# Scale and offset of X behind chosen loads, roped queries turned behind the keys, silu ahead of additions, first token tile finished first

## The chip, the cores and the metric

One Trainium2 chip, one core of it. The metric is the time of one execution on the device, in microseconds (us), as the median of several runs. The engines are TensorE (PE; its weight loads, PEld, overlap the matmuls), VectorE (DVE), ScalarE (ACT), GpSimd (POOL) and SyncE (SP), which only issues transfers.

## The reference

Two layers over 256 tokens of width 2048. Each mixes tokens with eight heads of latent attention and 1024 channels of causal convolution side by side, projects both with one matrix, and then applies a squared-ReLU MLP of width 8192. A layer norm stands before the layers and after each half of a layer.

```python
def hybrid_layer(x, cos, sin, ...):
    z = x @ w_in
    c_q, c_kv, k_rope, u = z[..., :o1], z[..., o1:o2], z[..., o2:o3], z[..., o3:]
    q = (rms_norm(c_q, g_q) @ w_uq).reshape(B, S, MLA_HEADS, QK_NOPE + QK_ROPE)
    q_nope = q[..., :QK_NOPE]
    q_rope = apply_rope(q[..., QK_NOPE:], cos[:, :, None, :], sin[:, :, None, :])
    kv = (rms_norm(c_kv, g_kv) @ w_ukv).reshape(B, S, MLA_HEADS, QK_NOPE + V_HEAD)
    k_nope, v = kv[..., :QK_NOPE], kv[..., QK_NOPE:]
    k_rope = apply_rope(k_rope, cos, sin)
    attn = chunk_causal_mla(q_nope, q_rope, k_nope, k_rope, v).reshape(B, S, MLA_WIDTH)
    u = u + b_glu
    h = u[..., :CONV_WIDTH] * jax.nn.sigmoid(u[..., CONV_WIDTH:])
    h = causal_depthwise_conv(h, w_dw, b_dw)                 # 31 taps
    h = jax.nn.silu(layer_norm(h, g_cln, b_cln))
    mix = jnp.concatenate([attn, h], axis=-1) @ w_out
    x = layer_norm(ALPHA * x + mix, ln1_g, ln1_b)
    f = jnp.square(jax.nn.relu(x @ w1)) @ w2
    return layer_norm(ALPHA * x + f, ln2_g, ln2_b)

def reference(x, ...):
    h = layer_norm(x, ln_in_g, ln_in_b)
    for l in range(DEPTH):
        h = hybrid_layer(h, ...)
    return h
```

## The kernel before

X, the activations, stays in SBUF as two token tiles (t = 0, 1) of 128 tokens by 2048; a block n of it is 512 columns. All weights come from HBM once, in chunks of up to 1 MB, in the order of `chunk_order` (line 193): per layer the convolution inputs u(0) to u(3), between them the query and key/value latents (zq, zk), the roped and plain query parts (qr, qn), keys (kn), values (v), then the projection wo in two halves (k0 = 0 takes the attention result mx, k0 = 8 the convolution result mc), then w1 and w2.

Each matmul in fp32 is made of three with operands cut into a high and a low part. So a chunk is loaded into `wr` (`load_next`, line 234, SP's queue), ACT rounds it to `wh` (line 264) and VectorE or GpSimd subtracts to get the low half `wl` (line 265, which is line 93 where VectorE does it). `gpsimd_low` (line 42) says whose work it is: GpSimd's for most of what lies before the MLP. A chunk is 24 matmuls of 512 columns for `wo` (12 a token tile) and 48 of 256 columns for u. `get` and `retire` pace loads and cuts by what TensorE has used up: a few chunks ahead (`ahead`), at most `cap` loaded and not given back.

The program text isn't the order of the queues. The compiler of this language simulates all engines and puts each instruction into its engine's queue when it would be ready there; after that each queue runs in order, and an instruction that waits holds what stands behind it. `tc.issue_after(ins)` puts the instructions of its block behind `ins` where they are on the same engine. It does nothing else.

The places that matter here:

- **The input norm** (`class First`, line 470). Its scale and offset are first applied to the transposed copy only (`gain`). `rest(n)` (line 491) applies them to X itself later, for the sum after the projection: for scale and then offset it issues a broadcast of 512 numbers to all partitions on SP and two GpSimd operations on X. It is called for n = 0 to 3 after the key rope, within the keys, after the values and after the attention of layer 0 (lines 853, 923, 928, 999).
- **rstd_of** (line 354) makes each norm's reciprocal root: a VectorE step (vi, vq, vk, vc, va, vb), then a power on GpSimd (ri, rq, rk, rc, ra, rb).
- **Latents** (`rms_T`, line 778): squares on ACT, `rstd_of`, the normalised latents `cnq` on VectorE, turned by TensorE (cTq).
- **query_rope** (line 870): VectorE ropes the queries of each token tile into `rt`, TensorE turns them (qrT). It stands before the plain queries and the keys (`keys`, line 882).
- **conv_norm** (line 1013): the convolution output is turned, normalised (`yt`, after rc), turned back in four groups (`cp`, yT), and ACT and VectorE make the silu and cut it into mc. It is written before blocks 2 and 3 of the projection's first half.
- **close** (line 701): the last part of a sum, with the statistics of the following norm. In its last block token tile 0 is done first, `between` starts tile 0's norm, then tile 1 runs; the norm of tile 1 follows. Block 2 of tile 0, and blocks 1 to 3 of tile 1 (in the very last norm block 3 alone), are scaled on ACT and GpSimd (`nrm`, line 393); the rest is two VectorE operations on X.
- **PSUM banks** (lines 122 to 150): ring `mm` for sums, `ax` for turnings, two for the convolution. In the MLP `mm` has six.

## Time and profile before

| | |
|---|---|
| median of 3 runs | 2053.14 us (2051.37 to 2055.04) |
| profiled execution, on the device | 2048.13 us |
| its span, first to last instruction | 2046.3 us |
| TensorE busy | 1995.7 us (98%) |
| VectorE, ACT, GpSimd busy | 1235.9, 949.2, 361.6 us |
| moved by DMA | 377.67 MB, 185 GB/s in the mean |

Times in the rows below are from the span's start. Layer 0 runs from about 48 to 1035 us; the MLPs of both layers fill most of the span. A matmul's row shows its modelled length; matmuls overlap, so the rate is read from a stretch with their count.

### The profile page before, as it was taken

What the parts mean: (1) busy time and instruction counts of PE and PEld (TensorE: products, weight loads), DVE (VectorE), ACT (ScalarE), POOL (GpSimd) and SP (SyncE); (2) the same over time, 40 slices, a digit from 0 to 9 for tenths busy, and PEclk for the clock granted to TensorE, in tenths of its full rate; (3) what the DMA queues carried; (4) which work ended last, traced back from release to release, by engine and by line L of the source; (5) the groups of instructions that cost most, each with busy time, mean ns of one, the idle gap of its engine ahead of it and who ended that gap; (6) DMA issues with size and microseconds to landing.
All of it is one profiled execution on the core that took longest, in us unless ns stands there. A gap on an engine that the chain in (4) does not pass through costs nothing. (4 is left out here: it accounts for less than half of the span.)

```text
span 2046.3 us, 26177 instructions
## 1 busy us (share of the span) xinstructions
PE 1995.7 (98%) x10542; PEld 1706.2 (83%) x10542; DVE 1235.9 (60%) x1709; ACT 949.2 (46%) x1343; POOL 361.6 (18%) x224
## 2 busy tenths in 40 slices
PE   8899999999999999999999999999999999999997
PEld 5799877888888888888879997788888888888886
DVE  6776677554555555456567746875555545555564
ACT  5446555543453354345345564554444434543441
POOL 6496602000000000000038763200000000000001
PEclk8899999999999999999999999999999999999999
DMA  8565645566556645656556455455664565556561
GB/s 249 154 177 163 206 167 180 169 196 202 177 185 197 220 159 185 215 170 246 170 165 176 125 183 206 165 185 168 202 220 151 188 202 186 186 187 225 197 213 62
DMA packets 226170, 377.67 MB, mean 185 GB/s; under 512 B 15955, under 2 KB 70083, under 8 KB 225025
## 3 DMA queue, kind: packets, MB, share of 16 engines
q1 hardware_dynamic: 225696, 375.47, 56.3%
q8 instruction: 82, 1.34, 0.3%
q10 hardware_dynamic: 352, 0.54, 0.1%
q14 instruction: 40, 0.32, 0.1%
HBM read 373.88 MB, written 2.10 MB: 184 GB/s over the span
## 5 line engine op out<-in xcount | busy, mean ns | idle before, releaser
L264 ACT CAST wh<-wr 128x1024 fp32r<-128x1024 f32 (+2 forms) x700 | 684.8, 1031 | 727.9 <-DVE wl L93 323.3
L93 DVE TENSOR_TENSOR wl<-wr,wh 128x1024 fp32r<-128x1024 f32 x576 | 686.4, 1235 | 432.7 <-ACT wh L264 299.1
L93 PE MATMUL f<-xTa,wh 128*128 128x512 f32 x1920 | 676.8, 397 | 0.0
L93 PE MATMUL w<-wh,h 128*128 128x512 f32 x2048 | 632.2, 389 | 2.5 <-DVE f115s L93 1.4
L93 PE MATMUL f<-xTa,wl 128*128 128x256 f32 x1920 | 538.0, 281 | 0.0
L93 PEld LDWEIGHTS w<-wh,h 128*128 128x128 f32 x2048 | 384.4, 188 | 83.1 <-DVE f115s L93 1.7
L93 PEld LDWEIGHTS f<-xTa,wh 128*128 128x128 f32 x1920 | 360.4, 188 | 87.6
L93 PE MATMUL w<-wl,h 128*128 128x512 f32 x1024 | 398.4, 389 | 0.0
L93 PEld LDWEIGHTS f<-xTa,wl 128*128 128x128 f32 x1920 | 362.7, 189 | 0.9
L265 POOL TENSOR_TENSOR wl<-wr,wh 128x1024 fp32r<-128x1024 f32 (+2 forms) x124 | 268.2, 2187 | 92.8 <-ACT wh L264 44.4
L358 POOL TENSOR_TENSOR rb<-vb,mhalf 128x1 f32<-128x1 f32 x4 | 4.2, 1049 | 1396.8 <-DVE nmub L93 1396.8
L93 PEld LDWEIGHTS w<-wl,h 128*128 128x128 f32 x1024 | 192.2, 188 | 39.6
L93 DVE SCALAR_TENSOR_TENSOR cv<-hg,wdT,cv 128x255 f32<-128x255 f32 (+14 forms) x480 | 187.1, 466 | 9.3 <-ACT cv L639 9.3
L93 PE MATMUL wo<-wh,mc 128*128 128x512 f32 x256 | 82.6, 402 | 3.5 <-ACT mc L171 3.5
L93 PE MATMUL wo<-wh,mx 128*128 128x512 f32 x256 | 82.0, 396 | 1.1 <-ACT mx L171 1.1
L93 DVE TENSOR_TENSOR X<-X,w 128x512 f32<-128x512 f32 x48 | 33.0, 688 | 68.0 <-PE w L93 67.9
L93 PE MATMUL u<-xTi,wh 128*128 128x256 f32 x384 | 72.5, 289 | 0.3 <-DVE rbk L93 0.3
L93 PE MATMUL u<-xTb,wh 128*128 128x256 f32 x384 | 71.1, 286 | 0.0
L93 PEld LDWEIGHTS wo<-wh,mc 128*128 128x128 f32 x256 | 49.6, 194 | 15.0 <-ACT mc L171 4.5
L93 PEld LDWEIGHTS u<-xTi,wh 128*128 128x128 f32 x384 | 61.3, 195 | 0.7 <-DVE rbk L93 0.6
L93 PEld LDWEIGHTS u<-xTb,wh 128*128 128x128 f32 x384 | 60.2, 191 | 0.2
L93 PEld LDWEIGHTS wo<-wh,mx 128*128 128x128 f32 x256 | 47.8, 188 | 11.5 <-ACT mx L171 1.5
(400 smaller groups left out, 1837.0 us busy)
## 6 DMA issues: line engine op xcount, KB each, us to landing
wr<-in_w_dram SPq DMA_DIRECT2D x256, 1024.0 KB, 5.2
wr<-in_w_out_dram SPq DMA_DIRECT2D x32, 1024.0 KB, 5.4
wr<-in_w_in_dram SPq DMA_DIRECT2D x60, 512.0 KB, 6.1
wr<-in_w_in_dram SPq DMA_DIRECT2D x8, 1024.0 KB, 10.4
wr<-in_w_uq_dram SPq DMA_DIRECT2D x24, 256.0 KB, 4.3
wr<-in_w_in_dram SPq DMA_DIRECT2D x8, 640.0 KB, 4.4
wr<-in_w_ukv_dram SPq DMA_DIRECT2D x8, 512.0 KB, 5.1
wr<-in_w_in_dram SPq DMA_DIRECT2D x16, 128.0 KB, 5.1
```

The source lines that it names most:

```text
L93: return f(*args, **kw)
L264: nc.scalar.copy(hi[:, c], raw[:, c])
L265: eng.tensor_sub(lo[:, c], raw[:, c], hi[:, c].bitcast(F32))
L358: nc.gpsimd.tensor_tensor(out=r, in0=v, in1=mhalf, op=ALU.pow)
```

## The change

- `gpsimd_low`: the low halves of layer 0's first u group are VectorE's, no longer GpSimd's.
- `rest`: called later (after the values, after u(3), and twice within the projection's first half); its broadcasts issue behind the latest weight load, its GpSimd operations behind GpSimd's latest low half at that place of the program.
- The roped queries of token tile 0 are turned behind the last matmul of the keys' first half, those of tile 1 behind the second.
- Projection, first half, block 3: the second chunk's matmuls for token tile 0 issue behind the turning of silu group 1, those for tile 1 behind that of group 2; the block's additions issue behind the cut of group 1 on VectorE.
- Projection, second half: blocks 2 and 3 are interleaved so that token tile 0 is finished first. Token tile 0 of block 3 ends 36 matmuls before the end; it was 24.
- The very last sum: token tile 1 is added up in PSUM (four banks, `end`) and normalised from there; of its blocks GpSimd takes block 2 and not block 3.

```diff
     if tag == "u":
-        return key[2] >= 2 - l or (l, key[2]) == (0, 0)
+        return key[2] >= 2 - l
...
-                nc.sync.dma_start(sl(rv), ap)
+                last["load"] = nc.sync.dma_start(sl(rv), ap)
...
-                eng.tensor_sub(lo[:, c], raw[:, c], hi[:, c].bitcast(F32))
+                low = eng.tensor_sub(lo[:, c], raw[:, c], hi[:, c].bitcast(F32))
+                if eng is nc.gpsimd:
+                    last["low"] = low
...
+        def source(self, t, n):
+
+            return self.inp.get((t, n), X[:, t, n * 512:(n + 1) * 512])
...
-                eng.scalar_tensor_tensor(out=X[:, t, c], in0=X[:, t, c], scalar=m[:, 0:1], in1=self.g[:, c],
+                eng.scalar_tensor_tensor(out=a, in0=a, scalar=m[:, 0:1], in1=self.g[:, c],
                                          op0=ALU.subtract, op1=ALU.mult)
-                eng.scalar_tensor_tensor(out=X[:, t, c], in0=X[:, t, c], scalar=r, in1=self.b[:, c],
+                eng.scalar_tensor_tensor(out=X[:, t, c], in0=a, scalar=r, in1=self.b[:, c],
                                          op0=ALU.mult, op1=ALU.add)
...
-                nc.sync.dma_start(w, ap[c].partition_broadcast(P))
-                for t in range(2):
-                    nc.gpsimd.tensor_tensor(out=X[:, t, c], in0=X[:, t, c], in1=w, op=op)
+                with tc.issue_after(last["load"].ins):
+                    nc.sync.dma_start(w, ap[c].partition_broadcast(P))
+                with tc.issue_after(last["low"].ins):
+                    for t in range(2):
+                        nc.gpsimd.tensor_tensor(out=X[:, t, c], in0=X[:, t, c], in1=w, op=op)
...
+        elif t and N is not None and N.last:
+            vector.tensor_add(ps[t], X[:, t, c], ps[t])
+            N.inp[t, n] = ps[t]
         else:
             vector.tensor_add(X[:, t, c], X[:, t, c], ps[t])
...
+            pc, pd = out_banks(tag, l, k0, 2), [psum(f"{tag}{l}_{k0}_3_0")]
+            out_part(pc, tag, l, k0, 2, 0, act, False)
+            out_part(pc, tag, l, k0, 2, 1, act, True, (0,))
+            accumulate(0, pc, 2, first, N)
+            for kc in range(2):
+                out_part(pd, tag, l, k0, 3, kc, act, kc == 1, (0,))
+            between(0, pd)
+            pd.append(psum(f"{tag}{l}_{k0}_3_1"))
+            out_part(pc, tag, l, k0, 2, 1, act, True, (1,))
+            accumulate(1, pc, 2, first, N)
+            out_part(pd, tag, l, k0, 3, 0, act, False, (1,))
+            out_part(pd, tag, l, k0, 3, 1, act, True, (1,), lambda: between(1, pd))
+            accumulate(1, pd, 3, first, N)
         N.head(1)
-        for n in range(3 if N.last else 1, NC4):
-            N.nrm(1, n, nc.gpsimd)
+        for n in range(1, NC4):
+            if not N.last or n == 2:
+                N.nrm(1, n, nc.gpsimd)
...
-        beside(query_rope())
+        def query_turn(t, after):
+            ps = psumx(f"qrT{l}{t}")
+            with tc.issue_after(after.ins):
                 for k in range(4):
-                    tensor.transpose(ps[:, k * P:(k + 1) * P], rt[:, k * P:(k + 1) * P], ident)
-                nc.scalar.copy(qr[:, :, t * P:(t + 1) * P], v3(ps, 4))
+                    tensor.transpose(ps[:, k * P:(k + 1) * P], rt[t][:, k * P:(k + 1) * P], ident)
+            nc.scalar.copy(qr[:, :, t * P:(t + 1) * P], v3(ps, 4))
+        query_rope()
...
         queries(0)
-        keys(0)
-        if l == 0:
-            N.rest(1)
-        keys(4)
+        query_turn(0, keys(0))
+        query_turn(1, keys(4))
         values(0)
         values(1)
         if l == 0:
-            N.rest(2)
+            N.rest(0)
         queries(4)
...
         beside(attention((0, 1, 2, 3)))
+        u_group(3)
         if l == 0:
-            N.rest(3)
-        u_group(3)
+            N.rest(1)
...
         out_part(pa, "wo", l, 0, 0, 1, mixT, True)
+        if l == 0:
+            N.rest(2)
...
+        if l == 0:
+            N.rest(3)
+        flush()
+        beside(conv_norm())
+        ps = out_rows("wo", l, 0, 2, mixT)
+        for t in range(2):
+            accumulate(t, ps, 2, True)
+        ps = out_banks("wo", l, 0, 3)
+        out_part(ps, "wo", l, 0, 3, 0, mixT, False)
+        with tc.issue_after(turned[1].ins):
+            out_part(ps, "wo", l, 0, 3, 1, mixT, True, (0,))
+        with tc.issue_after(turned[2].ins):
+            out_part(ps, "wo", l, 0, 3, 1, mixT, True, (1,))
+        with tc.issue_after(silus[1].ins):
             for t in range(2):
-                accumulate(t, ps, n, True)
+                accumulate(t, ps, 3, True)
...
-                give_back()
+                if N.last:
+                    banks["end"] = banks["mm"][2:]
+                    del banks["mm"][2:]
+                else:
+                    give_back()
                 close("w2", l, q * 16, act, N)
```

## Rows read from the trace of the kernel before

**Rows 1.** The page: busy us, share of the span, instructions, by engine.

```profile
PE 1995.7 (98%) x10542; PEld 1706.2 (83%) x10542; DVE 1235.9 (60%) x1709; ACT 949.2 (46%) x1343; POOL 361.6 (18%) x224
```

**Rows 2.** Waits of TensorE: waiter <- releaser: us in total, times, longest.

```profile
PE cTq L93 <- DVE cnq L93: 9.4, 1, 9.4
PE tri L93 <- DVE xv L93: 5.7, 3, 3.4
PE qrT L93 <- DVE rt L93: 4.8, 2, 2.4
PE wo L93 <- ACT mc L171: 3.5, 4, 1.2
PE f L93 <- DVE xTa L93: 2.2, 2, 1.1
PE yT L93 <- ACT zz L1041: 1.8, 2, 0.9
PE u L93 <- POOL wl L265: 1.6, 2, 0.9
...
PE tra L93 <- DVE X L93: 1.2, 2, 0.6
```

**Rows 3.** VectorE's timeline: start, us, line, operation, count, idle before.

```profile
74.38 0.14 DVE L93 TENSOR_SCALAR vq<-ssq 128x1 f32<-128x1 f32 x1
...
85.72 0.75 DVE L93 SCALAR_TENSOR_TENSOR cnq<-zq,rq,gq 128x512 f32<-128x512 f32 x1 [7.47 <-POOL rq L358]
```

**Rows 4.** GpSimd's timeline, same columns, 58 to 96 us.

```profile
58.66 3.66 POOL L497 TENSOR_TENSOR X<-X,gi 128x512 f32<-128x512 f32 x2 [9.55 <-DMA gi<-in_ln_in_g_dram]
...
82.67 2.48 POOL L497 TENSOR_TENSOR X<-X,bi 128x512 f32<-128x512 f32 x2 [4.07 <-DMA bi<-in_ln_in_b_dram]
85.11 0.57 POOL L358 TENSOR_TENSOR rq<-vq,mhalf 128x1 f32<-128x1 f32 x1
```

**Rows 5.** Stretches: engines' busy us (instructions), granted clock, DMA share, GB/s.

```profile
86.62:90.10 3.48, 3.48 (x17) 3.48 (x18) 2.95 (x7) 0.59 (x1) 1.79 (x2) 0.50 0.18 58
...
271.00:274.40 3.40, 3.40 (x9) 2.61 (x8) 2.54 (x3) 3.39 (x6) 0.00 (x0) 0.50 0.09 33
```

**Rows 6.** GpSimd's timeline, first half of layer 0's projection.

```profile
232.53 19.03 POOL L265 TENSOR_TENSOR wl<-wr,wh 128x1024 fp32r<-128x1024 f32 x8 [3.82 <-ACT wh L264]
254.81 1.07 POOL L358 TENSOR_TENSOR rc<-vc,mhalf 128x1 f32<-128x1 f32 x2 [3.25 <-DVE vc L93]
```

**Rows 7.** Stretch of the first half of the projection, wo alone.

```profile
233.94:251.10 17.16, 17.16 (x75) 14.00 (x75) 2.73 (x4) 1.00 0.92 311
```

**Rows 8.** TensorE's timeline at the roped queries and at the silu.

```profile
160.13 0.66 PE L93 MATMUL qrT<-ident,rt 128*128 128x128 f32 x4 [2.38 <-DVE rt L93]
...
267.29 0.60 PE L93 MATMUL yT<-ident,yt 128*128 128x128 f32 x4
```

**Rows 9.** Stretch of one half of the keys, instructions on kn alone.

```profile
160.98:163.90 2.92, 2.92 (x24) 2.87 (x25) 0.21 (x1) 1.00 0.51 123
```

**Rows 10.** VectorE's timeline, the convolution norm's last output.

```profile
257.44 1.52 DVE L93 TENSOR_SCALAR yt<-cT,cmv,rc 128x512 f32<-128x512 f32 x2
```

**Rows 11.** VectorE's timeline at the end.

```profile
2036.39 2.07 DVE L93 SCALAR_TENSOR_TENSOR X<-X,mvb,gb 128x512 f32<-128x512 f32 x3
2038.38 4.08 DVE L93 SCALAR_TENSOR_TENSOR X<-X,rb,bb 128x512 f32<-128x512 f32 x3
```

**Rows 12.** GpSimd's timeline at the end.

```profile
2038.37 1.87 POOL L403 TENSOR_TENSOR X<-X,gb 128x512 f32<-128x512 f32 x1 [0.83 <-ACT X L402]
2040.32 1.59 POOL L404 TENSOR_TENSOR X<-X,bb 128x512 f32<-128x512 f32 x1
```

**Rows 13.** VectorE's timeline in the head.

```profile
19.12 5.91 DVE L93 TENSOR_SCALAR X<-X,mvi,ri 128x512 f32<-128x512 f32 x4 [0.68 <-POOL ri L358]
...
44.31 2.36 DVE L93 TENSOR_TENSOR wl<-wr,wh 128x1024 fp32r<-128x1024 f32 x2 [5.71 <-ACT wh L264]
```

**Rows 14.** ACT's timeline at the end of the head.

```profile
43.23 2.00 ACT L264 CAST wh<-wr 128x1024 fp32r<-128x1024 f32 x2 [6.89 <-DMA wr<-in_w_in_dram]
```

More of the change, by code (lines that the diff above doesn't have):

```diff
@@ L230, in hybrid_trunk @@
     index = {k: i for i, (k, _) in enumerate(plan)}
-    raws, ready, cut_after = {}, {}, {}
+    raws, ready, cut_after, last = {}, {}, {}, {}
     state = dict(loaded=0, cut=0, retired=0, ahead=1, cap=5, hold=False, gate=None, pieces=2)
@@ L330, in stat_w @@
                              skip_group_check=True)
-            tensor.matmul(o, lhsT=lo[:, ki, c], rhs=act[:, 0:S], start=False, stop=last,
-                             skip_group_check=True)
+            done = tensor.matmul(o, lhsT=lo[:, ki, c], rhs=act[:, 0:S], start=False, stop=last,
+                                 skip_group_check=True)
+        return done
     def stat_w2(o, hi, lo, ki, m, act, first, last):
@@ L365, in __init__ @@
             self.mv = {}
+            self.inp = {}
             self.done = set()
@@ L652, in out_banks, with out_part @@
     def out_banks(tag, l, k0, n):
-        return [psum(f"{tag}{l}_{k0}_{n}_{t}") for t in range(2)]
-    def out_part(ps, tag, l, k0, n, kc, act, last, tokens=(0, 1)):
+        return [turns(f"{tag}{l}_{k0}_{n}_{t}", "end" if t and "end" in banks else "mm") for t in range(2)]
+    def out_part(ps, tag, l, k0, n, kc, act, last, tokens=(0, 1), amid=None):
         hi, lo = get(tag, l, k0, n, kc)
@@ L663, in out_part @@
                         retire(tag, l, k0, n, kc)
+                    if amid is not None and ki == 1:
+                        amid()
                     tick()
@@ L711, in between @@
                 N.turn(0, 0)
-        for n in range(NC4):
-            end = n == NC4 - 1
-            ps = out_rows(tag, l, k0, n, act, (3 if N.last else 2) if end else 0, between)
-            for t in range(2):
-                if t or not end:
-                    accumulate(t, ps, n, first, N)
+        if len(act) > 2:
+            for n in range(NC4):
+                end = n == NC4 - 1
+                ps = out_rows(tag, l, k0, n, act, (3 if N.last else 2) if end else 0, between)
+                for t in range(2):
+                    if t or not end:
+                        accumulate(t, ps, n, first, N)
+        else:
+            for n in range(NC4 - 2):
+                ps = out_rows(tag, l, k0, n, act)
+                for t in range(2):
+                    accumulate(t, ps, n, first, N)
+            pc, pd = out_banks(tag, l, k0, 2), [psum(f"{tag}{l}_{k0}_3_0")]
[11 more added lines that the diff above has]
+            accumulate(1, pd, 3, first, N)
         N.head(1)
-        for n in range(3 if N.last else 1, NC4):
-            N.nrm(1, n, nc.gpsimd)
+        for n in range(1, NC4):
+            if not N.last or n == 2:
+                N.nrm(1, n, nc.gpsimd)
     for l in range(L):
@@ L851, in hybrid_trunk @@
         beside(key_rope())
-        if l == 0:
-            N.rest(0)
         u_group(2)
@@ L868, in hybrid_trunk @@
         retire("qr", l)
+        rt = []
         def query_rope():
             for t in range(2):
[L872 to L875 removed]
+                rt.append(work(f"rt{l}{t}", "ev", 4))
+                rope(v3(rt[t], H), v3(pq[t], H), t, H, f"q{l}{t}")
+        def query_turn(t, after):
+            ps = psumx(f"qrT{l}{t}")
+            with tc.issue_after(after.ins):
                 for k in range(4):
[L877 to L880 removed]
+                    tensor.transpose(ps[:, k * P:(k + 1) * P], rt[t][:, k * P:(k + 1) * P], ident)
+            nc.scalar.copy(qr[:, :, t * P:(t + 1) * P], v3(ps, 4))
+        query_rope()
         def keys(h0):
@@ L1011, in cuts_after @@
                 cut_after[i] = ins
+        turned, silus = [], []
         def conv_norm():
@@ L1042, in conv_norm @@
                                          scale=pH[:, l, 16 + c:17 + c])
+                turned.append(tr)
                 yield 1
@@ L1064, in hybrid_trunk @@
             accumulate(t, pb, 1, True)
-        for n in range(2, NC4):
-            if n == 2:
-                flush()
-                beside(conv_norm())
-            ps = out_rows("wo", l, 0, n, mixT)
+        if l == 0:
[3 more added lines that the diff above has]
+        ps = out_rows("wo", l, 0, 2, mixT)
+        for t in range(2):
+            accumulate(t, ps, 2, True)
[6 more added lines that the diff above has]
+        with tc.issue_after(silus[1].ins):
             for t in range(2):
-                accumulate(t, ps, n, True)
+                accumulate(t, ps, 3, True)
         flush()
```

27 lines of the change are left out of this document (13 added, 14 removed).

## The prediction

> **What bounds the kernel now.** The first view is the page: TensorE is busy 1995.7 us, 98% of the span of 2046.3 us [rows 1]. No other engine comes near, and the matrix work itself is not touched by the change, so all there is to win is time in which TensorE waits, stretches in which it works at its lower clock, and the ends. The second view is the list of TensorE's waits [rows 2]. One is long, 9.4 us in a single piece before the turned query latents (cTq). Behind it come three waits for xv at the start (5.7 us), two of 2.4 us for the roped queries (4.8 us), 3.5 + 1.8 us where the silu of the convolution half feeds the projection, 2.2 + 1.2 us between projection and MLP, and 1.6 us for low halves made by GpSimd. The third views are the timelines around each, to see who was late and why. The last is the end, where TensorE has nothing left and the rest is VectorE, GpSimd and the output [rows 11, 12].
>
> The profiled execution took 2048.13 us, 1.8 us more than its span and 5.0 us less than the median of the runs, 2053.14 us. The sum below is made against the profiled execution; the same difference is then taken off the median.
>
> **Scale and offset of X (the rest calls).** The cause of the 9.4 us is on GpSimd. VectorE has the variance sum (vq) ready at 74.38 us [rows 3], but the tiny power (rq, 0.57 us) runs at 85.11 us, because the multiply and add of X by scale and offset stand before it in GpSimd's queue and wait there for their broadcasts, up to 9.55 us for one [rows 4]. Afterwards TensorE works at half clock: granted 0.50, the 1.2 GHz level, from 86.62 to 90.10 us [rows 5]. Work that takes 3.48 us there takes 1.74 at the other level. The change puts each of the eight broadcasts behind a given weight load and the sixteen GpSimd operations behind a given low half, far later. rq can then start at 74.5 and end near 75.1, the normalised latents (cnq, 0.75 us [rows 3]) near 75.9 plus what VectorE is in the middle of, which is before TensorE asks at 77.2 (86.62 less 9.41). Gain: 9.4 + 1.7 = 11.1 us. With GpSimd rid of this work, its low halves for the u group behind the key/value latents no longer run late, and the 1.6 us [rows 2] go too.
>
> What was moved must now be paid somewhere: sixteen operations at 1.24 us (2.48 for two, [rows 4]), 19.8 us of GpSimd, half before the projection, where nothing close by waits for it, half within the first half of layer 0's projection. There GpSimd makes eight low-half operations back to back, 19.03 us from 232.53 [rows 6], so it ends at 251.56. Projection matmuls go at 17.16 / 75 = 0.229 us [rows 7], so the last of the eight weight chunks, 24 matmuls, is begun at 267.29 - 5.5 = 261.8 [rows 8]. The lead is 10.2 us, the added work there 8 x 1.24 = 9.9. It fits, barely, if no broadcast is late. Behind it in the queue is the power of the convolution's norm (rc, now at 254.81 [rows 6]) and behind that the transposes. I price this at 2 us, between 0 and the 9.9 of the rival below, nearer to 0 because rc can be queued between two low halves.
>
> **Roped queries.** TensorE stands 2.38 us before the second turning in each layer [rows 8], waiting for VectorE's rope. Now the turnings come after the first and second half of the keys. One half is 24 matmuls, 2.92 us [rows 9], more than the wait. The keys' low half and latents are older than the rope. Gain 4.8 us in all; if the keys were late, 0. The scores use the turned queries only after the values; that slack I read from the order of the code.
>
> **Silu.** After the last projection matmul of the attention half TensorE turns the convolution output at 267.29 us [rows 8], then waits for ACT, 1.8 us in all before transposes and 3.5 us before the matmuls on the silu's result, over both layers [rows 2]; and from 271.0 the clock granted is 0.50 for 3.40 us [rows 5], 1.7 us lost; there are two such stretches, one a layer. The convolution norm's output is there at 258.96 (257.44 + 1.52 [rows 10]), but part of the transposes sit behind all of the matmuls. Now the second pair is turned before the last quarter-block of 12 matmuls of token tile 0 and the third before those of tile 1, so ACT has two times 12 x 0.229 = 2.7 us of cover more; and VectorE must do the silu before it adds the last projection block. The bank that this addition frees is next written 12 matmuls into the new half, so the wait is covered. Full gain 5.3 + 3.4 = 8.7; less the 2 us above, 6.7. Bounds: 8.7, and below nothing, as the rivals tell, because TensorE can now be held by a transpose whose input is late.
>
> **Projection, token tile first.** The two blocks of the second half are reordered so that all of token tile 0 ends 36 matmuls before the end and not 24: 2.7 us more for its addition, statistics and scaling. The waits for it are 1.2 us (X) and 2.2 us (xTa) [rows 2]. I take 2.4 of the 3.4, since VectorE must still turn to token tile 1 in the same stretch; bounds 0 and 3.4. One weight chunk is given back 24 matmuls later, 5.5 us; the loads that this holds up on SP are those of the MLP's third chunk, used over 5 us after the end.
>
> **The tail.** Three additions of the offset take 4.08 us where three multiplications took 2.07 [rows 11], while GpSimd works on X beside them (1.87 and 1.59 us [rows 12], against 1.24 undisturbed). With tile 1's sum kept in PSUM, VectorE reads one operand there. By [rows 11] six operations of 0.69 from 2036.39 end at 2040.5, not 2042.5; GpSimd at its undisturbed speed ends at 2038.37 + 2.48 = 2040.9, not 2041.9. The later of the two is 2040.9, gain 1.5 us; bounds 0.5 (only the GpSimd end left) and 2.0. The third block goes to GpSimd in place of the fourth, with no effect on the sum. The Trainium skill (SBUF — State Buffer, Who interferes with whom) says that a VectorE instruction with two SBUF inputs and a GpSimd instruction that reads SBUF exclude each other, and one with a single SBUF input does not. By that rule the whole 1.5 us come; the 4.08 against 2.07 agrees.
>
> **The head.** The sixteen low halves of the first u group go from GpSimd to VectorE. At 2.36 us for two of twice the size [rows 13] they cost 0.59 each, 9.4 us on an engine that is nearly full there. Against it, VectorE's own operations slow beside GpSimd: four scalings of X took 5.91 us, 1.48 each [rows 13], where 0.59 is the price of a clean operation of that size with one input more. That gives back 3.6 us on these four, and as much is likely on the other four and on the eight splits. So the two nearly cancel. Bounds: gain of the 5.7 us of waits for xv [rows 2], or a loss of 9.4. I take a gain of 1, near the middle, because ACT has to wait for the next weights until 43.23 us anyway [rows 14]. The Trainium skill (VectorE: DVE Perf Modes, Mode 2×_2P) gives such a scaling two results a cycle, an estimate of 0.27 us each; by it the relief would be 4.8 us on the same four and the sum 1 or 2 us lower. No row shows one without GpSimd beside it.
>
> **Sum.** 11.1 + 1.6 + 4.8 + 6.7 + 2.4 + 1.5 + 1.0 = 29.1 us. Profiled execution 2048.1 - 29.1 = 2019.0; median 2053.1 - 29.1 = **2024.0 us**.
>
> **The rivals.**
> - *GpSimd's moved work holds the projection.* All eight of its operations stand before rc: rc comes at 254.81 + 9.9 = 264.7, the norm's output at 268.9, and TensorE, now bound to those transposes at 261.8, waits 7.1 us; layer 0's silu gain (2.7 after the price) is gone as well. 2024 + 9.8 = 2034. For it: the lead of 10.2 against 9.9. Against: layer 1 has no such work, and rc can slip in earlier. Chance 0.17.
> - *The head pays.* VectorE gets no relief and TensorE waits for the low halves, 9.4 lost and not 1 won: 2034. For it: VectorE has hardly an idle moment there. Chance 0.11.
> - *The long stall only moves.* With cTq in time the next limit is the supply of weights: a second half-load of that stretch was issued late as well, behind the same broadcasts. If half of the 11.1 stays, 2030. Chance 0.08; it lies inside the range.
> - *Slower than before.* The broadcasts are issued from SP, behind weight loads that wait for buffers; GpSimd would stand before low halves as it stood before rq. Four broadcasts in layer 0's projection at 9.55 each and 9.9 of work are 48.1 us, less the lead of 10.2: 37.9 us lost, 2062. It decides against the change from 7.4 us a broadcast on (29.1 + 10.2 - 9.9 over four). Chance 0.05: the loads there run well ahead.
>
> **How the numbers follow.** Forecast 0.57, rivals 0.17, 0.11, 0.08, 0.05, something not seen 0.02. Low end: all waits named go, 11.1 + 1.6 + 4.8 + 8.7 + 3.4 + 2.0 + 5.7 = 37.3, so 2016, and 2 us less for the spread of the runs: 2014. High end: the first two rivals together, 2024 + 9.8 + 10.4 = 2044. About 0.2% (4 us) is what a measurement of this kernel can tell from no change. Faster: 0.92; same 0.02; slower 0.06.
>
> **What would show it.** Right: no idle time before cTq, rq within 2 us of vq; no clock of 0.50 near 87 and 271 us; no wait of qrT on rt; the offset additions at the end at 0.7 us. Wrong: TensorE waiting for wl from GpSimd or for yt near 260 us; xv or wl waits before 45 us longer than now; rest operations waiting for broadcasts with low halves behind them.

## The result and the profile after

The changed kernel takes **2028.7 us** (median of 4 runs, 2028.1 to 2029.9) beside 2052.3 us for the kernel before on the same chip (4 runs, 2050.8 to 2055.0). The ratio is 0.9884, with a 95% interval from 0.9867 to 0.9901: 23.6 us gained, where 29.1 were forecast. The time lies 4.7 us above the forecast of 2024.0.

The profiled executions stand closer together: span 2046.3 us before, 2027.7 us after, 18.7 us less. The profiled execution of before was 4 us faster than its median, that of after 1.2 us slower. So the sizes below, which come from the two traces, add up to 18.7; the other 4.9 us lie between these two executions and the medians.

TensorE is busy 1993.4 us and has the same work as before. The first six rows of the list of its waits (waiter <- releaser: us in total, times, longest):

```profile
engine line waited for: us in total, times, longest us
PE tri L93 <- DVE xv L93: 7.5, 2, 4.3
PE yT L93 <- ACT zz L1080: 2.2, 4, 0.9
PE prmT L93 <- ACT xv L497: 2.0, 1, 2.0
PE pv L93 <- ACT pts L1019: 1.9, 1, 1.9
PE f L93 <- DVE xTa L93: 1.6, 2, 1.0
PE w L93 <- DVE f015s L93: 1.5, 1, 1.5
```

Beside [rows 2], the long wait before cTq, the waits for the roped queries, for mc and for GpSimd's low halves are gone. The waits for xv have grown from 5.7 to 7.5 us, and two have come: prmT on ACT (2.0) and pv on ACT (1.9, before 0.2). The wait of yT on ACT has grown from 1.8 to 2.2.

The granted clock, in three stretches (busy us with instructions of each engine, then clock, DMA share, GB/s):

```profile
core 0: us, PE busy (x) PEld busy (x) DVE busy (x) ACT busy (x) POOL busy (x), PEclk, DMA share, GB/s
27.48:37.72 10.24, 6.25 (x21) 5.08 (x22) 9.37 (x21) 7.74 (x20) 2.90 (x8) 0.50 0.90 284
86.60:90.10 3.50, 3.50 (x32) 3.50 (x31) 2.95 (x8) 1.94 (x3) 1.55 (x2) 1.00 0.24 53
256.17:259.58 3.41, 3.41 (x10) 2.62 (x9) 2.68 (x4) 3.41 (x8) 0.00 (x0) 0.50 1.07 403
```

The stretch at 87 us, at 0.50 in [rows 5], has its 2.4 GHz back. But there is a new one of 10.2 us at the 1.2 GHz level (0.50) in the start, and one at the silu of layer 0 again. At the silu of layer 1 the clock stays at 1.00, where before had 0.52 from 1271.0 to 1274.4.

Where the 18.7 us came from is read by laying the start of the same matmuls in both traces side by side (us; the last column is what the stage ending there gave):

| first matmul on | before | after | difference | stage, change |
|---|---|---|---|---|
| zq, layer 0 | 48.08 | 53.75 | +5.7 | start: +5.7 |
| qr, layer 0 | 146.19 | 137.54 | -8.7 | cTq and u: -14.3 |
| wo on mx, layer 0 | 214.00 | 203.54 | -10.5 | roped queries, attention: -1.8 |
| hT, layer 0 | 351.09 | 340.49 | -10.6 | projection, silu: -0.1 |
| u, layer 1 | 1035.15 | 1025.34 | -9.8 | MLP: +0.8 |
| wo on mx, layer 1 | 1213.52 | 1201.91 | -11.6 | roped queries, attention: -1.8 |
| hT, layer 1 | 1350.25 | 1335.18 | -15.1 | projection, silu: -3.5 |
| TensorE's end | 2034.47 | 2017.75 | -16.7 | MLP: -1.7 |
| end of the span | 2046.35 | 2027.66 | -18.7 | tail: -2.0 |

**What came as forecast.** VectorE's timeline and then GpSimd's (start, us, operation, count, idle before), where [rows 3, 4] were:

```profile
74.94 0.15 DVE L93 TENSOR_SCALAR vq<-ssq 128x1 f32<-128x1 f32 x1
...
76.15 0.75 DVE L93 SCALAR_TENSOR_TENSOR cnq<-zq,rq,gq 128x512 f32<-128x512 f32 x1
```
```profile
75.18 0.57 POOL L361 TENSOR_TENSOR rq<-vq,mhalf 128x1 f32<-128x1 f32 x1 [26.61 <-DVE vq L93]
```

GpSimd is idle when vq comes, rq runs 0.24 us after vq starts, and cnq is there at 76.9; TensorE turns it at 79.97 without a wait. In the tail the three offset additions take 2.06 us on VectorE (4.08 in [rows 11]) and GpSimd's operation beside them 1.26 us (1.59 in [rows 12]):

```profile
2019.68 2.07 DVE L93 SCALAR_TENSOR_TENSOR w<-w,mvb,gb 128x512 f32<-128x512 f32 x3
2021.65 2.06 DVE L93 SCALAR_TENSOR_TENSOR X<-w,rb,bb 128x512 f32<-128x512 f32 x3
```
```profile
2022.72 1.26 POOL L413 TENSOR_TENSOR X<-X,bb 128x512 f32<-128x512 f32 x1
```

**What did not: the start.** Timelines of TensorE, VectorE, GpSimd and ACT:

```profile
24.06 1.11 PE L93 MATMUL tri<-ident,X 128*128 128x128 f32 x8
29.45 1.12 PE L93 MATMUL tri<-ident,X 128*128 128x128 f32 x4 [4.28 <-DVE xv L93]
...
34.29 0.40 PE L93 MATMUL prmT<-ident,gbr 80*128 80x80 f32 x1 [2.02 <-ACT xv L497]
...
53.75 0.48 PE L93 MATMUL zq<-wh,xTi 128*128 128x512 f32 x1
```
```profile
8.68 1.92 DVE L93 TENSOR_SCALAR X<-X,mvi,ri 128x512 f32<-128x512 f32 x4 [0.67 <-POOL ri L361]
...
23.46 1.92 DVE L93 TENSOR_SCALAR X<-X,mvi,ri 128x512 f32<-128x512 f32 x4 [2.84 <-POOL ri L361]
25.30 2.81 DVE L93 TENSOR_TENSOR wl<-wr,wh 128x512 fp32r<-128x512 f32 x4
28.04 3.90 DVE L93 TENSOR_SCALAR xv<-tri,gbT 128x128 f32<-128x128 f32 x12
```
```profile
19.50 1.63 POOL L609 TENSOR_SCALAR angles<-invf,posf 128x32 f32<-128x32 f32 x2 [1.31 <-DMA invf<-in_inv_freq_dram]
21.22 1.55 POOL L614 TENSOR_SCALAR angles<-angles 128x64 f32<-128x64 f32 x4
22.85 0.58 POOL L361 TENSOR_TENSOR ri<-vi,mhalf 128x1 f32<-128x1 f32 x1
```
```profile
31.29 1.28 ACT L629 ACT_TABLE_LOAD   x1
...
32.74 1.49 ACT L497 ACTIVATE xv<-tri,gbT 128x128 f32<-128x128 f32 x4
```

The relief is there: the second token tile's four scalings of X take 1.92 us (23.46), not 5.91 as in [rows 13]. But VectorE stands 2.84 us for ri, the power of the second token tile, because GpSimd, now without low halves, has taken up the angles of the positions, has waited for their data and has them ahead of ri. Then four low halves come ahead of the twelve xv for which TensorE waits 4.28 us, and on ACT the rope's table load comes ahead of another four.

Two things make up the 5.7 us. Up to zq TensorE waits 10.9 us in all (xv 7.5, prmT 2.0, xTi 1.4), 3.3 more than before (xv 5.7, xTi 1.1, X 0.8). The rest is the clock: at 0.50 TensorE is busy 5.39 us from 13.85 to 20.60 and 6.25 us from 27.48 to 37.72, before only 6.90 us from 12.00 to 21.70. At the other level such work takes half the time, so the 4.74 us more cost an estimated 2.4.

**And the projection of layer 0.** ACT, TensorE, GpSimd:

```profile
218.44 3.89 ACT L264 CAST wh<-wr 128x1024 fp32r<-128x1024 f32 x4 [3.27 <-DMA wr<-in_w_out_dram]
222.23 0.85 ACT L1019 COPY pts<-pT 128x384 f32<-128x384 f32 x2
```
```profile
222.75 0.92 PE L93 MATMUL pv<-pts,vv 128*128 128x256 f32 x4 [1.85 <-ACT pts L1019]
```
```profile
238.38 9.45 POOL L265 TENSOR_TENSOR wl<-wr,wh 128x1024 fp32r<-128x1024 f32 x4
247.79 2.55 POOL L508 TENSOR_TENSOR X<-X,bi 128x512 f32<-128x512 f32 x2
250.30 1.06 POOL L361 TENSOR_TENSOR rc<-vc,mhalf 128x1 f32<-128x1 f32 x2
```

ACT has four casts, which wait for weights, ahead of the copy that pv needs; before it had two there and two behind. And rc comes at 250.30, counted from the first matmul on mx 6.0 us later than in [rows 6] (46.8 after 203.54, there 40.8 after 214.00). Between the low halves stand operations on X, eight of them from 226.10 on.

**The silu** itself, in layer 1, where no GpSimd work was moved in:

```profile
1249.34 0.49 PE L93 MATMUL yT<-ident,yt 128*128 128x128 f32 x3
1250.72 0.44 PE L93 MATMUL yT<-ident,yt 128*128 128x128 f32 x2 [0.89 <-ACT zz L1080]
1251.63 0.44 PE L93 MATMUL yT<-ident,yt 128*128 128x128 f32 x2 [0.47 <-ACT zz L1080]
```

The transposes that the change puts ahead of the last projection matmuls stand in one cluster. The second half of a pair goes to the bank of which ACT still reads the first half, and no matmul lies between the two.

### The profile page after: what moved, and what is told of

Read it like the earlier page. It is cut to its first block, busy times and chain, and to the rows that moved or that the text cites. A ratio compares the mean times of both kernels' runs of the same rounds, so it can differ in the third digit from the quotient of the medians.

```text
span 2027.7 us, 26190 instructions
## 1 busy us (share of the span) xinstructions
PE 1993.4 (98%) x10542; PEld 1706.2 (84%) x10542; DVE 1224.7 (60%) x1725; ACT 947.7 (47%) x1341; POOL 332.4 (16%) x208
## 5 line engine op out<-in xcount | busy, mean ns | idle before, releaser
L93 DVE TENSOR_TENSOR wl<-wr,wh 128x1024 fp32r<-128x1024 f32 (+1 forms) x592 | 694.2, 1216 | 432.5 <-ACT wh L264 294.1
L265 POOL TENSOR_TENSOR wl<-wr,wh 128x1024 fp32r<-128x1024 f32 (+1 forms) x108 | 245.0, 2291 | 85.5 <-ACT wh L264 42.2
L93 PEld LDWEIGHTS wo<-wh,mx 128*128 128x128 f32 x256 | 48.7, 191 | 11.6 <-ACT mx L171 1.5
```

What stands on the lines that cost most here:

```text
L93: return f(*args, **kw)
L265: low = eng.tensor_sub(lo[:, c], raw[:, c], hi[:, c].bitcast(F32))
```

## Experiments

The changed kernel ran once more and eleven others beside it, in three groups and a last one, each group with its own runs of the kernel before (7 each, medians 2050.1 to 2051.0). Differences of 2 us between medians lie within the scatter, so the verdicts rest on places in the traces, one trace a kernel; the span is that of the profiled execution. Five kernels leave the start as the change made it (after, after_again, rest_early, turn_spread, close_old), and their zq begins between 53.75 and 54.84: up to 1.1 us there is scatter.

| run | us (median of 4) | ratio to before (95%) | span | zq begins |
|---|---|---|---|---|
| after_again | 2027.5 | 0.9888 (0.9873 to 0.9902) | 2025.4 | 53.83 |
| rest_only | 2038.7 | 0.9940 (0.9925 to 0.9955) | 2034.2 | 48.56 |
| lows_back | 2024.0 | 0.9871 (0.9855 to 0.9888) | 2020.8 | 48.67 |
| power_first | 2026.8 | 0.9885 (0.9871 to 0.9900) | 2024.3 | 52.86 |
| xv_first | 2027.8 | 0.9889 (0.9873 to 0.9906) | 2024.9 | 52.91 |
| casts_behind | 2025.1 | 0.9875 (0.9860 to 0.9890) | 2024.3 | 50.15 |
| half_lows | 2029.7 | 0.9900 (0.9884 to 0.9917) | 2028.0 | 53.50 |
| rest_early | 2025.5 | 0.9879 (0.9864 to 0.9893) | 2024.1 | 54.09 |
| turn_spread | 2023.0 | 0.9865 (0.9850 to 0.9880) | 2021.3 | 54.13 |
| close_old | 2026.7 | 0.9882 (0.9867 to 0.9897) | 2024.7 | 54.84 |
| early_lows_back | 2022.0 | 0.9860 (0.9845 to 0.9875) | 2019.9 | 48.48 |
| three_cures | 2019.5 | 0.9852 (0.9835 to 0.9868) | 2017.2 | 48.49 |

**The changed kernel once more (after_again).**

> The changed kernel itself, beside the next three on the same chip: 23 to 24 us under the kernel before, as in its first runs (2028.7 against 2052.3).

2027.5 against 2050.4: 22.9 us. Its span is 2.2 us shorter than that of after; 1.6 of these hang on the clock at one place, told in the last section. From the first matmul on mx to hT in layer 0 it is 2.6 us faster than before, where after is 0.1.

### The scale and offset of X alone

**rest_only**: the kernel before with the eight broadcasts and sixteen operations placed as in the changed kernel, and nothing else. The calls of `rest` move as in the change; that part is left out here.

```diff
 ...
-                nc.sync.dma_start(w, ap[c].partition_broadcast(P))
-                for t in range(2):
-                    nc.gpsimd.tensor_tensor(out=X[:, t, c], in0=X[:, t, c], in1=w, op=op)
+                with tc.issue_after(last["load"].ins):
+                    nc.sync.dma_start(w, ap[c].partition_broadcast(P))
+                with tc.issue_after(last["low"].ins):
+                    for t in range(2):
+                        nc.gpsimd.tensor_tensor(out=X[:, t, c], in0=X[:, t, c], in1=w, op=op)
```

> The kernel before with one part of the change alone: the broadcasts of scale and offset and the sixteen GpSimd operations on X are placed as in the changed kernel. The prediction's account: the 9.4 us wait before cTq and the half-clock stretch behind it go (11.1 us) and the low-half waits of u go (1.6 us), 12.7 us in all, so 2052.3 - 12.7 = 2039.6 us; the start up to the first zq matmul (48.1 us) is that of before. Rival, that the moved work is paid for in layer 0's projection: the wait of pv on ACT (1.85 us) and of the projection on mx behind it, that the changed kernel shows near 221 us, appear here too, and the norm's power rc runs some 5 us later than in before when counted from the last attention transpose: 2 to 4 us given back, 2042 to 2044 us. Rival, that the long stall only moves: 2045 us.

2038.7 us, 11.9 under before; by the trace 12.1. Up to the first matmul on mx it is 13.3 us ahead. Then pv waits for pts, and the lead falls to 11.5 at the transposes of the convolution's sums (cT); rc comes at 247.23, 46.6 after the first matmul on mx (40.8 before).

```profile
219.72 0.92 PE L93 MATMUL pv<-pts,vv 128*128 128x256 f32 x4 [1.73 <-ACT pts L983]
```

So the main term holds (13.3 for 12.7), and 1.9 of it are given back by cT. They don't stay lost: at the first matmul on mc the lead is 10.7, but at hT, in the MLP, 13.0 again. In this trace no stretch at 0.50 follows the silu of layer 0 (before: 271.00 to 274.40, 1.7 us) and the second wait for mc is 0.41 us (before 1.16). The long stall did not move on to the weights: no wait of a u or zk matmul on a transfer stands in its list.

**rest_early**: the changed kernel with the last three quarters of this work one stage earlier.

```diff
         queries(4)
+        if l == 0:
+            N.rest(1)
 ...
+        if l == 0:
+            N.rest(2)
         u_group(3)
         if l == 0:
-            N.rest(1)
+            N.rest(3)
 ...
-        if l == 0:
-            N.rest(2)
 ...
-        if l == 0:
-            N.rest(3)
```

> The changed kernel with the last two quarters of the scale and offset work one stage earlier: the second quarter behind the last queries, the third behind attention, the fourth behind the last u group, so that none stands within the projection. Theory: that work delays the low halves of the projection and the norm's power rc (250.3 us, some 5.5 us later than before when counted from the end of attention), so that TensorE meets yt too early, waits 1.15 us in three pieces near 254 us and drops to half clock from 256.2 to 259.6 us. Here rc comes near 245 us, those waits and that stretch go: 1.15 + 1.7 = 2.9 us, 2025.8 us; with the 1.85 us wait of pv on ACT gone as well, 2024.0 us. Rival, that the order of ACT's casts makes pv wait and that it is not GpSimd's work: the 1.85 us stay. Rival, that the wait for the banks of yT (on zz from ACT) sets the pace there, not yt: time within 1 us of 2028.7.

The span falls from 2027.7 (2025.4 in after_again) to 2024.1. GpSimd's eight low halves stand together again and the first rc runs at 245.76, 41.9 us after the first matmul on mx (46.8 in the changed kernel); ACT has two casts ahead of pts and two behind:

```profile
218.61 2.00 ACT L264 CAST wh<-wr 128x1024 fp32r<-128x1024 f32 x2 [2.58 <-DMA wr<-in_w_out_dram]
220.51 0.85 ACT L1021 COPY pts<-pT 128x384 f32<-128x384 f32 x2
221.25 2.00 ACT L264 CAST wh<-wr 128x1024 fp32r<-128x1024 f32 x2
```

The wait of pv is gone, 2.05 us between the first matmul on mx and cT. The whole stage, from mx to hT, is 3.7 us shorter than in after and 1.2 shorter than in after_again. The edit moves nothing but the calls of `rest`, and ACT's order changes with them: the rival that this order has a cause of its own falls. Each call holds two broadcasts on SP and four operations on GpSimd; which of the two pushes the casts ahead of pts wasn't parted. The waits of yT stay, 0.89 and 0.47 us as in layer 1, but no stretch at 0.50 follows them: the last rival of the expectation (ACT's reading sets the pace) holds for these waits, the theory for the rest.

### The start

**lows_back**: one line.

```diff
     if tag == "u":
-        return key[2] >= 2 - l
+        return key[2] >= 2 - l or (l, key[2]) == (0, 0)
```

> The changed kernel with the sixteen low halves of the first u group given back to GpSimd. If moving them is what made the start longer (the first zq matmul at 53.75 us against 48.08 before), zq begins near 48.1 us here and the time is 2028.7 - 5.7 = 2023.0 us. If the start is longer for another cause (other transfers, the order of the rest), zq stays near 53 us and the time near 2028.7. If the move did help where VectorE's scalings of X got faster (1.92 us for four against 3.81 and 5.91), something of that is lost: 2024 to 2026 us.

zq begins at 48.67 and the span is 2020.8. The four scalings of X are slow again beside GpSimd, and it doesn't matter:

```profile
19.42 5.90 DVE L93 TENSOR_SCALAR X<-X,mvi,ri 128x512 f32<-128x512 f32 x4 [0.67 <-POOL ri L361]
25.25 3.91 DVE L93 TENSOR_SCALAR xv<-tri,gbT 128x128 f32<-128x128 f32 x12
```

xv begins at 25.25, in the changed kernel at 28.04. So the move of the low halves is what costs the start 5.1 us. Why, is not told by this run.

**power_first**: GpSimd's angles behind ri.

```diff
 ...
-            angles_within_pi()
+            with tc.issue_after(power1.ins):
+                angles_within_pi()
```

> The changed kernel with one order more: GpSimd's work on the angles of the positions is held behind the power of X's second token tile (ri). In the changed kernel ri runs at 22.85 us though its input is there at 19.42 us, because angle operations that waited for their data until 19.50 us stand before it, and VectorE stands 2.84 us for ri. Theory one, the order on GpSimd: VectorE's scaling of the second tile begins near 20.3 and not 23.46 us, TensorE's 4.3 us wait for xv shrinks by about 3 us, zq begins near 50.7 us, 2025.6 us. Theory two, the load on VectorE (9.4 us of low halves in front of xv): the 3 us are taken up by low halves that now come in ahead, zq stays within 1 us of 53.75, 2028 us. Theory three, the rope tables on ACT (1.28 us of table load ahead of xv, TensorE waits 2.0 us): that wait stays in both, and goes only where the tables come later.

VectorE's scaling begins at 21.23 (23.46) and the wait for xv falls from 4.28 to 2.70, yet zq begins at 52.86, only 0.9 earlier, which is no more than the scatter there. Theory one has the cause of that wait but not the sum: the tables, now later on ACT, wait 4.38 us for the angles there, with eight xv behind them, and TensorE waits 1.35 us for xTi and 1.27 us for ut. The 2.0 us wait before prmT is gone, as theory three had it, and it too came back elsewhere.

**xv_first**: as power_first, the tables behind the last split of X, and the low halves of chunks 2 and 3 (counted from 0) behind xv.

```diff
+                if state.get("behind") is not None:
+                    order.enter_context(tc.issue_after(state["behind"].ins))
                 low = eng.tensor_sub(lo[:, c], raw[:, c], hi[:, c].bitcast(F32))
 ...
     for n in range(1, NC4):
+        state["behind"] = last["xv"] if n > 1 else None
 ...
-            rope_tables()
+            with tc.issue_after(N.cut[0].ins):
+                rope_tables()
```

> The changed kernel with three orders at its start and nothing else: GpSimd's angles behind the power of the second token tile (as in the run power_first), the rope tables on ACT behind the last split of X, and VectorE's low halves of the third and fourth weight chunk behind the twelve scalings (xv) that TensorE's transposes wait for. Theory of order: it was not the 9.4 us of low halves on VectorE that cost the start 5 us, but where they stood. The wait for xv near 25 us (4.3 us in the changed kernel, 2.7 in power_first) falls under 1 us and zq begins at 49.5 to 50.5 us (53.75 and 52.86 there, 48.1 before): 3 to 4 us under the changed kernel. Theory of load: the low halves are late by what xv is early, TensorE waits the same 2 to 3 us for wl or for the split of X behind it, zq stays at 52 to 54 us.

```profile
26.55 0.66 PE L93 MATMUL tri<-ident,X 128*128 128x128 f32 x4 [1.03 <-DVE xv L93]
29.39 0.80 PE L93 MATMUL u<-wh,xTi 128*128 128x512 f32 x1 [2.19 <-ACT xTi L171]
```

zq at 52.91: by the number the theory of load, by the mechanism neither. The wait for xv has gone down to 1.03, nearly as forecast, but the new one is on ACT, whose half of the split stands behind four casts of the last chunk, at 26.64, that wait 0.76 us for their weights. From 28.2 to 38.2 us the clock is 0.50, with TensorE busy for 8.20 us: an estimated 4.1 us lost.

**casts_behind**: these casts, and their low halves, behind the split.

```diff
     for n in range(1, NC4):
         state["behind"] = last["xv"] if n > 1 else None
+        state["gate"] = cut10 if n > 2 else None
```

> The kernel of the run xv_first with one more order at the start: ACT's casts of the fourth weight chunk, and its low halves, behind the split of X's second token tile. In xv_first the wait for xv fell from 4.1 to 1.0 us, but TensorE then stood 2.19 us for ACT's half of that split (xTi), which was queued on ACT behind four casts that waited for their weights, and zq began at 52.91 us (48.1 in the kernel before, 53.8 in the changed one). Theory of order: with the casts behind it this wait goes and no half-clock stretch follows at 28 us; zq begins at 48.5 to 50 us. Theory of load (one engine does the low halves that two shared): TensorE waits elsewhere, for the low halves of the third and fourth chunk, zq at 52 to 53 us.

zq at 50.15. The wait of 2.19 is down to 0.22; 0.62 for xv and 0.93 for an xv of ACT have come. Between 22 and 30 us TensorE does 32 instructions, nearly as many as lows_back (34), where the changed kernel did 20. Four orders on three engines (angles, tables, low halves, casts) took 3.6 of the 5.1 us back with all low halves still on VectorE. Behind the new waits the clock does fall, against the expectation. From 30 to 38 us, casts_behind and then lows_back:

```profile
30.00:38.00 8.00, 7.47 (x29) 5.36 (x30) 7.22 (x12) 6.17 (x16) 7.75 (x4) 0.79 0.92 300
30.00:38.00 8.00, 8.00 (x36) 6.37 (x35) 5.87 (x6) 6.64 (x17) 7.83 (x6) 1.00 0.91 298
```

The low stretch is 31.20 to 34.62, TensorE busy 3.38 us; at the other level that would be an estimated 1.7 us less, about what is still missing against lows_back.

**half_lows**: power_first with chunks 2 and 3 back on GpSimd.

```diff
-        return key[2] >= 2 - l
+        return key[2] >= 2 - l or (l, key[2], key[3] > 1) == (0, 0, True)
```

> The kernel of the run power_first with the low halves of the third and fourth chunk of the first u group back on GpSimd and those of the first two on VectorE. Theory of load: eight of the sixteen low halves cost VectorE nothing in the stretch that counts, xv begins near 23.5 us, the wait for xv is 0 to 1 us, zq begins near 49 us. Theory of order on ACT: the split of X's second tile still stands behind the casts of the fourth chunk there, TensorE waits about 2 us for it at 27 us as in xv_first, and zq begins near 52 us although VectorE has been relieved.

```profile
29.05 0.50 PE L93 MATMUL u<-wh,xTi 128*128 128x512 f32 x1 [2.78 <-ACT xTi L171]
...
53.16 0.69 PE L93 MATMUL uT<-ident,ut 128*128 128x128 f32 x2 [3.52 <-DVE ut L93]
```

VectorE is relieved, and yet zq begins at 53.50, as late as in the changed kernel. The wait for ACT's split is there, as the theory of order said, 2.78 us. The 3.52 us are a wait that neither theory had: the rope tables, free to move again, and two table loads of 1.28 us each stand on ACT ahead of the tanh that ut needs. Without it zq would be near 50, by an estimate. So what the start loses is mostly order, which of several in-order queues holds the piece that TensorE asks for next, and the lower clock that follows such waits. The last 1.5 us of casts_behind (50.15 against 48.67) are about the size of its low stretch; whether the waits ahead of that come from load or from an order not tried stays open.

### Silu and the order of the projection

**turn_spread**: rest_early, with the second halves of pairs 0 and 1 turned behind 6 and 9 of the last 24 matmuls on mx.

```diff
 ...
-        with tc.issue_after(turned[1].ins):
-            out_part(ps, "wo", l, 0, 3, 1, mixT, True, (0,))
-        with tc.issue_after(turned[2].ins):
-            out_part(ps, "wo", l, 0, 3, 1, mixT, True, (1,))
 ...
+        for t, ki in [(t, ki) for t in range(2) for ki in range(4)]:
+            with tc.issue_after(spread["tr"].ins):
+                spread["mm"] = stat_x(ps[t], hi, lo, ki, mixT[1][:, ki], t, False, ki == 3)
+            if (t, ki) in ((0, 1), (0, 2), (0, 3)):
+                next(norm)
 ...
```

> The kernel of the run rest_early with the turning of the convolution output spread: the first halves of pairs 0 and 1 are turned ahead of the last 24 matmuls of the attention half, their second halves behind 6 and 9 of these, where the changed kernel turns them in one cluster and waits 0.89 and 0.47 us in each layer for ACT to read the first half out of the same bank. Theory: half of the silu gain that was forecast is lost in that cluster, since no matmul stands between a bank's two halves; here the two waits go in both layers, 2 x 1.36 = 2.7 us under rest_early. Rival, that ACT's time for the eight halves (0.92 us each) sets the end of the silu in any order: the matmuls on mc wait instead for what the transposes don't, within 0.7 us of rest_early.

```profile
1243.77 0.38 PE L93 MATMUL yT<-ident,yt 128*128 128x128 f32 x2
...
1246.07 0.38 PE L93 MATMUL yT<-ident,yt 128*128 128x128 f32 x2
...
1246.98 0.38 PE L93 MATMUL yT<-ident,yt 128*128 128x128 f32 x2
```

No idle time before any of these, in layer 1. The span is 2021.3, 2.8 us under rest_early. Of this 1.7 come in layer 1 and 1.0 in layer 0, where TensorE now meets yt too early and waits 0.49 us for it. The waits in the cluster were a loss of their own, and ACT's total was not the limit. The Trainium skill (PSUM — Partial Sum Buffer, Summary: rules for kernel authors) advises to read PSUM in another bank than the one that a matmul writes. The kernel keeps to that with waits, 1.36 us a layer in rest_early, until matmuls filled them.

**close_old**: rest_early with the old order of the projection's last two blocks.

```diff
-        if len(act) > 2:
+        if len(act) > 1:
```

> The kernel of the run rest_early with the projection's last two blocks in the old order (both token tiles of a block together, token tile 0 done 24 matmuls before the end and not 36). The prediction gave the new order 2.4 us over both layers. The traces so far show the waits behind the projection (X before the transposes, xTa before the MLP) at 1.69 us a layer before and 1.03 us in rest_early: a gain of 0.66 us a layer, 1.3 in all, so this run should be 1.3 us of span slower than rest_early, 2025.4. If the prediction's size was right, 2.4 slower. If the waits went down for another cause, no difference.

The span is 0.65 us longer, but zq already begins 0.75 later. From the first matmul on mc to the MLP's second matrix it loses 0.04 us in layer 0, and in layer 1 from the first matmul on mc to TensorE's end 0.09. So the new order is worth some 0.1 us a layer. The waits named are indeed shorter with it, 1.21 against 1.71 us in layer 1 (the expectation's 1.03 leaves out one of 0.18), but the time is not. With the new order the MLP's first matmul comes 0.6 to 0.7 us later behind the first on mc, and from there to hT 0.8 us are won back; why, wasn't followed further.

### The cures together

**early_lows_back** is rest_early with the one line of lows_back; **three_cures** is turn_spread with that line.

> The two cures that each worked alone, together: the low halves of the first u group on GpSimd as before the change, and the scale and offset work one stage earlier. If the two are independent their gains add in the trace (6.9 and 3.6 us of span under the changed kernel, of which the 2.2 us of a half-clock stretch and a wait for low halves are in both): 8.3 us under the changed kernel, a span near 2019.4 us. If the earlier GpSimd work collides with the low halves of the first groups, less.

A span of 2019.9 (2019.4 expected), 2022.0 us. A wait of pv is back, 0.20 us (0.48 in three_cures).

> The changed kernel with all three things that helped in the runs so far: low halves of the first u group back on GpSimd, scale and offset work one stage earlier, the turning of the convolution output spread between the last matmuls of the attention half. early_lows_back has the first two (span 2019.9, median 2022.0); turn_spread took 2.8 us of span off rest_early. If this adds up: a span of 2017.1 and a median of 2019.2 us, a ratio of 0.985 to the kernel before. If the spread turning depended on where rest_early left ACT and GpSimd, less than 2.8.

A span of 2017.2 and 2019.5 us, ratio 0.9852 (0.9835 to 0.9868). It is the fastest kernel of this case, 8.0 to 9.2 us under the changed one by the medians, 8.2 to 10.5 by the spans. The first rows of its list of waits:

```profile
PE tri L93 <- DVE xv L93: 4.7, 3, 2.5
PE tri L93 <- DVE X L93: 1.7, 2, 0.8
PE f L93 <- DVE xTa L93: 1.2, 2, 0.6
```

## Why the prediction was right, and where it was wrong

The sign and the main term were right, and the time lies in the range. By the traces 18.7 us came where 29.1 were summed up. The shortfall of 10.4 has two large parts, the head (6.7) and the silu with the new order of the projection (5.5), and smaller terms went both ways. By the medians it is only 5.5. Part of that closeness is luck: the medians count as gain the 4 us by which the profiled execution of before was faster than its median, and 0.9 us came in the MLPs that no term had.

- **Scale and offset (11.1 + 1.6).** Right: 14.3 us in that stage, 14.0 there in rest_only alone. Of the 1.6 more than summed, 0.3 is a wait for rbk that went as well; the rest wasn't followed. rq runs 0.24 us after vq starts, as forecast within 2 us. The rival that the stall only moves fell.
- **The price of the moved work (2).** The place was wrong: not rc ahead of yt but the casts on ACT ahead of pv, 1.9 us in rest_only. The size can't be called right, for it hangs on the clock behind it: by hT 0.3 us of it are left in rest_only, and in the same stage rest_early got back 1.2 against after_again, 3.7 against after. The first rival was half true. rc came 6.0 us later and TensorE did meet yt too early, but waited 0.28 us for it and not 7.1; the lead of 10.2 us that the prediction worked out held.
- **Roped queries (4.8).** The waits went, 2.4 us in each layer. 0.6 a layer were given back before the projection; 0.3 of that is a new wait of pT on ACT in the attention, the rest wasn't followed.
- **Silu (6.7).** Mis-sized. In layer 1, where no price was due, silu and new order together gave 3.5 of the 5.5 us that half of 8.7 and 2.4 make, an estimated 1.7 of them by the clock that no longer falls there. In layer 0 they gave 0.1 in after, where it falls, and 2.6 in after_again, where it doesn't. The step that failed: "ACT has two times 12 x 0.229 = 2.7 us of cover more". The cover lies behind the cluster of transposes, not between a bank's halves, where the waits arise. turn_spread put matmuls there and got 2.8 us.
- **Projection, token tile first (2.4).** Mis-sized: some 0.2 us in both layers (close_old). A wait that gets shorter was counted as time won.
- **The tail (1.5).** 2.0 us, the upper bound. By the rule of the Trainium skill (SBUF — State Buffer, Who interferes with whom) the additions with one SBUF input (outside the modes that use both ports) and GpSimd's operations don't slow each other; the trace agrees, 2.06 us for three and 1.26 for one. Token tile 0, left in SBUF, shows the contrast in the same trace: two such additions take 3.48 us from 2014.15 on, beside GpSimd.
- **The head (gain of 1).** Wrong sign: a loss of 5.7. The second rival came, at 5.7 instead of 9.4, and by another mechanism. The prediction weighed load against contention on VectorE, and got the relief right (5.91 to 1.92 us for four). It did not ask what GpSimd would do when freed (angles ahead of ri), nor what the new places of the low halves would push back on VectorE and on ACT, nor that a lower clock would follow the waits (an estimated 2.4 of the 5.7). power_first, xv_first and casts_behind show four such orders, worth 3.6 us together. "ACT has to wait for the next weights until 43.23 us anyway" was no cover: TensorE lost its time before that, and the next weights came little later (44.55).
- **Not in the sum.** A wait of 1.39 us for f115s at the last block of the MLP went, and one for f015s, in layer 0, grew by 0.42. rest_only still has the first (1.19 us), so it went through one of the parts of the change that rest_only leaves out; which one wasn't tried.

Of the signs of being wrong that the prediction named, three came, all small: a wait for yt at 253.90, of 0.28 us, longer waits for xv, and an operation on X that waits 1.30 us for its broadcast at 203.40 with a low half behind it. Of the signs of being right, the clock at the silu held in after_again and not in after. The time lies between the forecast and the first two rivals together (2044), since both rivals came at a fraction of their price.

## What to carry to other kernels

GpSimd, relieved of its low halves, did not stay idle here: what the scheduler put in their place went into the same in-order queue, ahead of the small operation that others waited for. So for each piece of work that is moved away, look at what moves up, on that engine and on those that share its inputs. And look at the granted clock behind each new wait: in the start it cost an estimated 2.4 us beside 3.3 of waits. Cover is worth something only between the two instructions that wait for each other: say for each wait which matmuls will stand in exactly that gap, and measure a gain by the start of a later matmul, not by the length of the wait.

## What the runs showed that was not expected

- **The same waits, with and without a slower clock.** In after and in casts_behind the waits of 1.15 us in three pieces at the silu of layer 0 are followed by 3.4 us at 0.50 (256.17 to 259.58 in after); in after_again, lows_back, power_first and xv_first the same pieces (0.28, 0.39 to 0.40, 0.47) are followed by full clock. So are 2.34 us in four pieces in rest_only. Both traces of the changed kernel run the same program, and 1.6 us between their spans hang on this; what decides it stays open.
- **Scalings beside GpSimd.** Four scalings of X by TENSOR_SCALAR take 1.92 us, 0.48 each, both with GpSimd on small angles (23.46 in after) and with GpSimd idle, as those of the first token tile in after, at 8.68, when GpSimd does nothing from 8.64 to 18.00. Beside GpSimd's low halves they take 5.90 (lows_back). The Trainium skill (VectorE: DVE Perf Modes, Mode 2×_2P) had led to an estimate of 0.27 us each without GpSimd, from the results a cycle alone; the measurement, 0.48, decides. In half_lows three splits of xTi, two SBUF inputs each, take 4.44 us beside GpSimd's low halves, where one takes 0.68 in after with GpSimd idle.
- **Moving half was no better than moving all.** half_lows (0.9900, 0.9884 to 0.9917) can't be told from the changed kernel (0.9888, 0.9873 to 0.9902), through a place that the edit doesn't touch: the table loads ahead of ut.
